# A two-layer encoder trunk on one core: first weight in two halves, some LayerNorm work on ScalarE, another order of head groups, and a table of priority shifts

## The chip, the cores and the metric

The kernel runs on one core of a Trainium2 chip. A core has a matmul engine (TensorE, PE in the profile), an elementwise engine (VectorE, DVE), an activation engine (ScalarE, ACT), a general engine (GpSimd, POOL) and an engine that here only issues DMAs (SyncE, SP). Each engine works through its own queue of instructions in order, and the engines wait for each other by semaphores. Matmul results land in PSUM, everything else lies in SBUF. The metric is the device time of one execution in microseconds (us); less is better.

## The reference

The input x is 512 rows (tokens) of 1024 values, in float32. After one LayerNorm come two layers, each with three kinds of attention side by side and a gated MLP:

```python
proj = x @ w_in                                   # 1024 x 4608
# differential softmax attention: 4 heads, two softmaxes of width 64 each,
#   rotary on 16 of 64 dims; o = (p0 - lam * p1) @ v, then rms_norm
# HGRN2 gated linear recurrence: 4 heads, 128 x 128 state, forward and backward,
#   summed, rms_norm, times silu(gate)
# cross-attention into 256 memory rows: 4 heads of 128
mix = jnp.concatenate([da_o, hg_o, mx_o], axis=-1) @ w_out
x = layer_norm(DEEPNORM_ALPHA * x + mix, ln1_g, ln1_b)
u = depthwise_conv_centred(x @ w_up, conv_w, conv_b)   # width 3 over the rows
gate, val = jnp.split(u, 2, axis=-1)
x = layer_norm(DEEPNORM_ALPHA * x + (jax.nn.silu(gate) * val) @ w_down, ln2_g, ln2_b)
```

The output is the 512 x 1024 result of the second layer.

## The kernel before

**Matmuls.** A float32 operand is split into a high and a low float16 part, and a product is three float16 matmuls (`mm3`: high x high, high x low, low x high). x lies transposed in `xh` and `xl` (8 blocks of 128 channels by 512 rows), the residual row-wise in four tiles `z[0]` to `z[3]` of 128 rows each.

**Weights.** `prep` brings one weight tile (1 MB, for the MLP's up-projection 512 KB) into SBUF: a DMA into one of two buffers `wst` (L302, or L300 in two pieces), the sum of squares on ScalarE (L307), a matmul with ones into a column of `stat` (L168), a power of two from the result's exponent on VectorE (`we`, `ws`, `wi`: L155 to L159), the scaled high part on ScalarE (`wh`, L310) and the low part on VectorE (`wl`, L311). The buffer `wst` is free when L311 is done, and only then the DMA of the next weight but one starts.

**Start.** `START` gives the order: constants, the first LayerNorm's gain and bias, the four tiles of x, two weights. `first_norm` takes each tile's mean and variance on VectorE (`norm`, L227 and L229), adds epsilon on GpSimd (L231), raises to the power -0.5 on GpSimd (L232) and normalises the tile on VectorE (L258). Then, for each block of 128 channels, four transposes on PE (L262), gain and bias on ScalarE (L264), high part and low part on VectorE (L265, L266). The first projection (`step_i`, the recurrence's values) has eight blocks of high-part matmuls, and then the matmuls with the weight's low part.

**A layer.** Head groups are worked on as pairs of heads: `hg` (recurrence), `mx` (memory) and `da` (differential), two pairs each. `SEQ` lists the order in which their projections and output projections are written into the program. Attention itself runs beside that in "lanes", stepped by the matmul time that the main line has used: recurrence and differential pairs share lane 0, memory pairs have lane 1. `rope_step` does the rotary part of the differential queries and keys on VectorE (L1003 to L1009). Output projections add into z through L569 (eviction of a PSUM bank, on VectorE). The last output projections are those of the memory pairs and of the second differential pair, and each finished row tile goes through `layernorm` (statistics L227 and L229, epsilon and power on GpSimd L231 and L232, L280 and L281 on VectorE, transposes L288, parts L292 and L293). The MLP runs in groups of up to four 128-column pairs, and after the last group `layernorm` runs again. With `idx == 4` (the last one) its result goes to the output by DMA (L283) instead of to transposes.

**Order.** The program is traced once, and `make_plan` reads its instructions, in the order in which they were written. `extract` finds what each depends on, and gives it a cost from a table of formulas; `deadlines` gives each a priority: a matmul the matmul time written before it, any other instruction the latest time at which those behind it can still be on time. The first `FIRST` DMAs come ahead of all. `simulate` then lists the instructions engine by engine: whenever an engine is free, the ready instruction with the smallest priority goes next. The program is traced a second time with these orders and with the buffers that the plan chose. The chip runs exactly these queues.

Of the kernel before, what the change touches and what calls it, by code (L numbers as in the profile page):

```python
# [10 lines left out]
F32 = mybir.dt.float32  # L11
F16 = mybir.dt.float16
# [27 lines left out]
MX_COST = 0.8  # L40
MX_EARLY = 4
START = "c0123wv"
_seq = [("hg", 0), ("rope",), ("hg", 1), ("mx", 0), ("mx", 1), ("da", 0), ("out", "hg", 0), ("da", 1), ("out", "hg", 1), ("out", "da", 0)]
SEQ = [_seq, _seq]
LANE = {"hg": 0, "da": 0, "mx": 1}
LAST = ("da", 1)
# [49 lines left out]
def trunk(ctx: ExitStack, tc: tile.TileContext, a, out, slots=None):  # L96
# [117 lines left out]
    qin = cp.tile([P, DEPTH], F32, name="qin")  # L214
    mkin = cp.tile([P, 2], F32, name="mkin")

    def load_x(t):
        nc.sync.dma_start(z[t], a["x"][0, t * P : (t + 1) * P, :])

# [2 lines left out]

    def norm(t, idx):
        zt = z[t]
        st = small(12, "bnst")
        for j in range(2):
            V.bn_stats(st[:, j * 6 : (j + 1) * 6], zt[:, j * 512 : (j + 1) * 512])  # L227
        mv = small(2, "bnmv")
        V.bn_aggr(mv, st)  # L229
        rs = small(1, "lnrs")  # L230
        G.tensor_scalar(rs, mv[:, 1:2], LN_EPS / (ALPHA * ALPHA if idx else 1.0), None, ALU.add)  # L231
        G.tensor_tensor(rs, rs, mhalf[:, 0:1], ALU.pow)  # L232
        return mv[:, 0:1], rs

# [20 lines left out]
    def first_norm():  # L255
        for t in range(TT):
            mu, rs = norm(t, 0)
            V.tensor_scalar(z[t], z[t], mu, rs, ALU.subtract, ALU.mult)  # L258
        for k in range(KT):
            pt = ptr()  # L260
            for t in range(TT):
                T.transpose(pt[:, t * P : (t + 1) * P], z[t][:, k * P : (k + 1) * P], ident)  # L262
            w = tmp([P, S], "w2", bufs=4)
            A.activation(w, pt, AF.Identity, scale=gbc[:, 0, k : k + 1], bias=gbc[:, 1, k : k + 1])  # L264
            V.tensor_scalar(xh[:, k, :], w, 1.0, None, ALU.mult)  # L265
            V.tensor_tensor(xl[:, k, :], w, xh[:, k, :], ALU.subtract)  # L266

# [24 lines left out]
                A.activation(xhs, pv, AF.Identity, scale=lnsc[:, idx : idx + 1])  # L292
                V.scalar_tensor_tensor(xls, pv, lnsc[:, idx : idx + 1], xhs, ALU.mult, ALU.subtract)  # L293

    def prep(src, shape):
        st = slot(wp, [P] + shape, F32, "wst", 2)
        if isinstance(src, tuple):
            w = shape[1] // len(src)
            for i, s_ in enumerate(src):
                nc.sync.dma_start(st[:, :, i * w : (i + 1) * w], s_)  # L300
        else:
            nc.sync.dma_start(st, src)  # L302
        n = shape[0] * shape[1]
        flat = st.rearrange("p a b -> p (a b)")
        h = slot(wp, [P] + shape, F16, "wh", 4)
        ss = small(1, "wss")
        A.activation(h.rearrange("p a b -> p (a b)").bitcast(BF16), flat, AF.Square, accum_out=ss)  # L307
        s, inv = pow2_scales(ss, 1, "w")
        l = slot(wp, [P] + shape, F16, "wl", 4)
        A.activation(h.rearrange("p a b -> p (a b)"), flat, AF.Identity, scale=s)  # L310
        V.scalar_tensor_tensor(l.rearrange("p a b -> p (a b)"), flat, s, h.rearrange("p a b -> p (a b)"), ALU.mult, ALU.subtract)  # L311
        return Weight(h, l, inv)

    def mm3(o, wh, wl, dh, dl, first, last, wt):
# [201 lines left out]
    def rms(o, eps=None):  # L516
        sq = tmp([P, 4, P], "w2", bufs=4)
        A.activation(sq, o.rearrange("p (c v) -> p c v", c=4), AF.Square)
        ss = small(4, "rmss")
        V.tensor_reduce(ss, sq, AX.X, ALU.add)  # L520
        rs = small(4, "rmrs")
        if eps is None:
            G.tensor_scalar(rs, ss, 1.0 / P, RMS_EPS, ALU.mult, ALU.add)
        else:
            G.tensor_tensor(rs, ss, eps, ALU.add)
        G.tensor_tensor(rs, rs, mhalf, ALU.pow)
        on = tmp([P, 4, P], "w2", bufs=4)
        V.tensor_tensor(on, o.rearrange("p (c v) -> p c v", c=4), rs.unsqueeze(2).broadcast_to([P, 4, P]), ALU.mult)
        return transposes(on)
# [66 lines left out]
    def emit():  # L596
        order = [(si, wi) for si, st in enumerate(steps) for wi in range(len(st[0]))]
        ready = {}
        at = [0]

        def prep_until(n):
            while at[0] < min(n, len(order)):
                si, wi = order[at[0]]
                spec = steps[si][0][wi]
                ready[si, wi] = prep(spec, [KT, 256] if isinstance(spec, tuple) else list(spec.shape[1:]))
                at[0] += 1

        done = set()
        cur = [None] * len(lanes)
        credit = [0.0] * len(lanes)  # L610

        def unit_step(i):
            if cur[i] is None:
                if not lanes[i] or not all(x in done for x in lanes[i][0][2]):
                    return None
                name, fn, _ = lanes[i].pop(0)
                cur[i] = (name, fn())
            try:
                return next(cur[i][1])
            except StopIteration:  # L620
                done.add(cur[i][0])
                cur[i] = None
                return 0.0

        def pump(dt):
            for i in range(len(lanes)):
                credit[i] += dt
                while credit[i] > 0:
                    c = unit_step(i)
                    if c is None:  # L630
                        credit[i] = 0.0
                        break
                    credit[i] -= c

        for op in START:
            if op == "c":
                ln_columns()
            elif op in "wv":
                prep_until("wv".index(op) + 1)
            else:  # L640
                load_x(int(op))
        seen = 0
        for si, (specs, fn, name, needs) in enumerate(steps):
            for x in needs:
                while x not in done:
                    if all([unit_step(i) is None for i in range(len(lanes))]):
                        raise RuntimeError(f"{x} can not run yet")
            seen += len(specs)
            prep_until(seen + AHEAD if specs else seen)
            t0 = pe_time[0]  # L650
            g = fn([ready.pop((si, wi)) for wi in range(len(specs))])
            if g is not None:
                for _ in g:
                    dt = pe_time[0] - t0
                    pump(dt)
                    t0 = pe_time[0]
            pump(pe_time[0] - t0)
            if name is not None:
                done.add(name)
# [32 lines left out]
    def build_layer(l):  # L692
# [55 lines left out]
        def hg_units(pr):  # L748
# [57 lines left out]
            def hg_attn():  # L806
# [31 lines left out]
                while m < S:  # L838
                    nb = S // m
                    for j in range(2):  # L840
                        Q, K, At, Dg, Tm = Qs[j], Ks[j], As[j], Ds[j], Ts[j]
                        p_ = psc()
                        if m <= 16:
# [7 lines left out]
                            V.copy_predicated(Dg, mk, p_[:, 0:P].rearrange("p (c t) -> p c t", c=4))  # L851
                            if m == 16:
                                for b in range(4):
                                    G.tensor_copy(diag_block(At, 32 * b, 32 * b, 32), Dg[32 * b : 32 * b + 32])
                        elif m <= 64:
                            for c in range(4):
                                for b in range(P // m):
# [364 lines left out]


class Op:
    __slots__ = ("i", "name", "eng", "cost", "tail", "reads", "writes", "table", "preds", "succs", "tiles", "dmab", "line", "kind", "small", "order_ins", "mv", "istr", "half", "mode")


def cost_of(i, kind, eng, outs, ins):
# [56 lines left out]
def extract(instrs):  # L1285
    ops = []
    last_half = None
    for i in instrs:
# [26 lines left out]
            o.cost, o.tail = cost_of(i, kind, o.eng, outs, ins)  # L1315
        o.reads = [b for b in ins if type(b.tensor).__name__ == "Tile"]
        o.writes = [b for b in outs if type(b.tensor).__name__ == "Tile"]
        o.preds, o.succs = set(), []
        o.small = _n(outs[0].ap) <= 16 if outs else False
        o.half = None  # L1320
        if o.eng == "PE":
# [42 lines left out]
    for o in ops:  # L1364
        o.tiles = []
        for wr, bs in ((False, o.reads), (True, o.writes)):
            for b in bs:
                t = b.tensor
                nm = t.name
                if nm not in tiles:  # L1370
                    tiles[nm] = t
                if nm not in o.tiles:
                    o.tiles.append(nm)
                psum = "PSUM" in str(t.space)
                p0, p1, m = region(b)
                h = hist[nm]
                for (j, w2, a0, a1, m2) in h:
                    if (wr or w2) and j != o.i:
                        if psum or (a0 < p1 and p0 < a1 and m & m2):
                            o.preds.add(j)  # L1380
        for wr, bs in ((False, o.reads), (True, o.writes)):
            for b in bs:
                p0, p1, m = region(b)
# [2 lines left out]
                if wr:  # L1386
                    if psum:
                        h[:] = []
                    else:
                        h[:] = [e for e in h if not (p0 <= e[2] and e[3] <= p1 and (e[4] & ~m) == 0 and e[0] != o.i)]  # L1390
                h.append((o.i, wr, p0, p1, m))
    for o in [o for o in ops if o.dmab][:FIRST]:
        o.dmab *= FAST
    gang, of = [], []
# [22 lines left out]
def simulate(ops, tiles, prio, fixed=None, wait=0.0, log=None):  # L1417
# [6 lines left out]
    free = {e: 0.0 for e in ("PE", "DVE", "ACT", "POOL", "SP")}  # L1424
    table = 0
    mode = 128
    dma_free = 0.0

    users = defaultdict(list)
    for o in ops:  # L1430
# [53 lines left out]
    while done < N:  # L1484
# [58 lines left out]
        order[e].append(i)  # L1543
        done += 1
        for s in o.succs:
            lat = LAT if ops[s].eng != o.eng else (0.03 if e != "PE" else -o.tail)
            if ops[s].eng == "POOL" and e != "POOL":
                lat += 0.12
            r = end[i] + lat
# [13 lines left out]
    return max(end), start, end, order, slot_of  # L1563


PEN = 20.0
SHARE = 0.35
TURN = 4.0
FIRST = 9
FAST = 205 / 370.0  # L1570


def deadlines(ops, tiles):
# [31 lines left out]
        D[i] = d  # L1605
    for k, o in enumerate([o for o in ops if o.dmab][:FIRST]):
        D[o.i] = k - 1000.0
    return [T[o.i] if o.eng == "PE" else D[o.i] for o in ops]


def make_plan(instrs):
# [48 lines left out]
```

## Time and profile before

| what | value |
|---|---|
| median of 3 runs | 1492.83 us (1492.78 to 1493.38) |
| the profiled execution, its own time | 1492.88 us |
| its span, first to last instruction | 1491.1 us |
| granted TensorE clock, mean | 0.997 of full |
| HBM read, written | 138.24 MB, 2.10 MB (94 GB/s over the span) |

The difference between time and span, 1.78 us, lies before the first and behind the last instruction. In the profile a group of instructions is named by engine, line, and the tiles that it writes and reads (`wl<-wst,ws,wh`). A row of the timeline begins with the start and the duration in us, and ends, in brackets, with the idle time before it and what ended it. A row of the windows view has the stretch, its length, and the busy time and number of instructions of each engine in it, then the granted clock, the DMA engines' busy share and GB/s. The page's 40 slices show VectorE's load over the span, in tenths:

```profile
DVE  7989968978997677666785978789888777566777
ACT  5876655666376556455466656566645656455550
```

### The profile page before, as it was taken

To read this page: it belongs to the slowest core of one execution; us is meant where nothing else is said; L and a number is where in the kernel's file an instruction comes from. 1 tells how busy PE (TensorE), PEld (TensorE's weight loads), DVE (VectorE), ACT (ScalarE), POOL (GpSimd) and SP (SyncE) were. 2 spreads that over 40 slices of the span, in tenths; PEclk is the share of its full clock that TensorE was granted. 3 is DMA by queue.
4 is the path that set the end of the run, shared out by engine and by line. 5 is a ranking of instruction groups with operands and counts; after the bars stand their busy time and mean duration, and the time that the engine had idled before them with its cause. 6 is when DMAs were issued, how large, how long until landed. Compare 5 with 4: busy or idle time off the path is not lost. (4 is left out here: it accounts for less than half of the span.)

```text
span 1491.1 us, 24496 instructions
## 1 busy us (share of the span) xinstructions
PE 1451.7 (97%) x9978; PEld 811.9 (54%) x9978; DVE 1168.4 (78%) x2242; ACT 865.1 (58%) x1094; POOL 130.1 (9%) x154
## 2 busy tenths in 40 slices
PE   6999999999999999999999999999999999999997
PEld 4566675565564444444487475655656544444443
DVE  7989968978997677666785978789888777566777
ACT  5876655666376556455466656566645656455550
POOL 1001020000111101001000101001001101001011
PEclk9999999999999999999999999999999999999999
DMA  6342111223143323232324202112232323333221
GB/s 238 114 150 86 59 58 59 101 71 101 46 143 114 107 85 113 85 113 96 128 90 140 87 30 86 57 57 77 79 100 85 113 88 118 99 92 114 86 84 57
DMA packets 158171, 141.91 MB, mean 95 GB/s; under 512 B 3302, under 2 KB 139114, under 8 KB 158058
## 3 DMA queue, kind: packets, MB, share of 16 engines
q1 hardware_dynamic: 158058, 140.35, 29.2%
q8 instruction: 78, 1.28, 0.3%
q14 instruction: 35, 0.29, 0.1%
HBM read 138.24 MB, written 2.10 MB: 94 GB/s over the span
## 5 line engine op out<-in xcount | busy, mean ns | idle before, releaser
L140 PEld LDWEIGHTS <-wh 128*128 128x128 f16 x2624 | 251.0, 98 | 237.5 <-issue 3.4
L311 DVE SCALAR_TENSOR_TENSOR wl<-wst,ws,wh 128x2048 f16<-128x2048 f32 x122 | 312.5, 2561 | 52.3 <-ACT wh L310 51.4
L140 PE MATMUL mm<-xh,wl 128*128 128x512 f16 (+1 forms) x832 | 305.3, 367 | 0.6 <-DVE wl L311 0.6
L140 PE MATMUL mm<-xh,wh 128*128 128x512 f16 (+1 forms) x832 | 305.2, 367 | 0.0
L140 PE MATMUL mm<-xl,wh 128*128 128x512 f16 (+1 forms) x832 | 305.0, 367 | 0.0
L307 ACT ACTIVATE wh<-wst 128x2048 bf16<-128x2048 f32 x122 | 232.2, 1903 | 102.4 <-PE stat L168 49.2
L310 ACT ACTIVATE wh<-wst,ws 128x2048 f16<-128x2048 f32 x122 | 243.5, 1996 | 40.1 <-DVE ws L157 19.5
L140 PE MATMUL mm<-wh,t 128*128 128x512 f16 (+1 forms) x768 | 223.5, 370 | 0.0
L140 PEld LDWEIGHTS <-wl 128*128 128x128 f16 x1312 | 128.2, 98 | 123.0 <-DVE wl L311 0.9
L140 PEld LDWEIGHTS <-t 128*128 128x128 f16 x1152 | 110.2, 98 | 121.4 <-issue 0.6
L569 DVE SCALAR_TENSOR_TENSOR z<-mm,inv,z 128x512 f32<-128x512 f32 x176 | 130.2, 745 | 45.9 <-PE mm L140 32.2
L140 PE MATMUL sc<-xl,wh 128*128 128x512 f16 (+1 forms) x416 | 147.5, 355 | 0.0
L140 PE MATMUL sc<-xh,wl 128*128 128x512 f16 (+1 forms) x416 | 147.5, 355 | 0.0
L140 PE MATMUL sc<-xh,wh 128*128 128x512 f16 (+1 forms) x416 | 147.5, 355 | 0.0
L140 PE MATMUL mm<-wl,t 128*128 128x512 f16 (+1 forms) x384 | 142.1, 370 | 0.0
L155 DVE TENSOR_SCALAR we<-stat 128x1 int32<-128x1 int32 x122 | 18.6, 153 | 118.8 <-PE stat L168 118.6
L1151 POOL TENSOR_TENSOR t<-f 128x512 f32<-128x512 f32 x44 | 60.6, 1378 | 542.7 <-DVE f L1149 438.6
L140 PE MATMUL mm<-wh,mgh 128*128 128x512 f16 x192 | 73.3, 382 | 4.7 <-DVE z L569 4.7
L1147 ACT ACTIVATE f<-sc,cvb,cw 128x512 f32<-128x512 f32 x44 | 34.1, 775 | 71.4 <-PE stat L168 69.3
L140 PE MATMUL mm<-wh,mgl 128*128 128x512 f16 x192 | 72.9, 381 | 0.9 <-DVE mgl L547 0.6
L140 PE MATMUL mm<-wl,mgh 128*128 128x512 f16 x192 | 73.3, 382 | 0.0
L1042 ACT ACTIVATE f<-sc,dam,iqk 128x512 f32<-128x512 f32 x64 | 49.3, 774 | 38.8 <-DVE dam L1040 34.3
(244 smaller groups left out, 2125.4 us busy)
## 6 DMA issues: line engine op xcount, KB each, us to landing
wst<-in_w_up_dram SPq DMA_DIRECT2D x88, 512.0 KB, 4.3
wst<-in_w_in_dram SPq DMA_DIRECT2D x36, 1024.0 KB, 4.8
wst<-in_w_down_dram SPq DMA_DIRECT2D x22, 1024.0 KB, 4.9
wst<-in_w_out_dram SPq DMA_DIRECT2D x12, 1024.0 KB, 4.9
wst<-in_w_mem_kv_dram SPq DMA_DIRECT2D x8, 1024.0 KB, 5.0
z<-in_x_dram SPq DMA_DIRECT2D x4, 512.0 KB, 4.9
mix<-in_ln_g_dram SPq DMA_DIRECT2D x4, 512.0 KB, 3.6
mix<-in_ln_b_dram SPq DMA_DIRECT2D x4, 512.0 KB, 4.7
```

Of the source, the lines that this page charges most:

```text
L140: T.matmul(o, lhsT, rhs, start=start, stop=stop)
L155: V.tensor_scalar(e, tot.bitcast(I32), 0x7F000000, 1, ALU.bitwise_and, ALU.logical_shift_right)
L307: A.activation(h.rearrange("p a b -> p (a b)").bitcast(BF16), flat, AF.Square, accum_out=ss)
L310: A.activation(h.rearrange("p a b -> p (a b)"), flat, AF.Identity, scale=s)
L311: V.scalar_tensor_tensor(l.rearrange("p a b -> p (a b)"), flat, s, h.rearrange("p a b -> p (a b)"), ALU.mult, ALU.subtract)
L569: V.scalar_tensor_tensor(zs, p_, ivs[half % len(ivs)], zs, ALU.mult, ALU.add)
L1042: A.activation(pe[:, c, :], sc_[c], AF.Exp, bias=mx[:, c : c + 1], scale=iqk, accum_out=z1 if c else z0)
L1147: A.activation(c, p_, AF.Identity, scale=cw[:, 1, v : v + 1], bias=cvb[:, l, i + 22 * v : i + 22 * v + 1])
L1151: G.tensor_tensor(gt[:, n, :], c2[:, 0, :], c2[:, 1, :], ALU.mult)
```

## The change

- The first weight is brought in by `prep_parts` in two halves of four blocks each: two DMAs, two sums of squares (their matmuls add up in one column of `stat`), two scaled high parts, two low parts. `FIRST` goes from 9 to 10 for it.
- `ACT_TILES = 1`: tile `z[0]` is normalised on ScalarE, with a small VectorE instruction for its bias.
- `ACT_STATS = (0, 0, 0, 0, 3)`: in the last LayerNorm the sum and the centred sum of squares of tiles 0 to 2 come from two ScalarE passes with accumulation instead of VectorE's L227 and L229.
- The epsilon additions of `norm` and `rms` go from GpSimd to VectorE. The copies of the recurrence's 32 x 32 blocks (L854) go from GpSimd to ScalarE. `DVE_BLOCKS` is empty and so does nothing. An ACTIVATE on a constant (`warm`) is written at the start.
- `SEQ`: the projections of the differential pairs come ahead of those of the memory pairs, and the output projections behind both.
- The planner: reads of one PSUM tile by one engine keep their order (`soft`); the DMA engines are taken to be free from 2.1 us on; and `deadlines` adds a table `NUDGE` of some 300 entries. An entry `(engine, a, b, d)` adds d us to the priority of that engine's instructions among those numbered a to b.

```diff
+FIRST_PARTS = 2
+ACT_TILES = 1
+ACT_STATS = (0, 0, 0, 0, 3)
+DVE_BLOCKS = ()
-_seq = [("hg", 0), ("rope",), ("hg", 1), ("mx", 0), ("mx", 1), ("da", 0), ("out", "hg", 0), ("da", 1), ("out", "hg", 1), ("out", "da", 0)]
+_seq = [("hg", 0), ("rope",), ("hg", 1), ("da", 0), ("da", 1), ("mx", 0), ("mx", 1), ("out", "hg", 0), ("out", "hg", 1), ("out", "da", 0)]
...
+    warm = cp.tile([P, 4], F32, name="warm")
+    A.activation(warm, mhalf, AF.Square)
...
     def norm(t, idx):
         zt = z[t]
+        if t < ACT_STATS[idx]:
+            sm = small(12, "bnst")
+            scr = tmp([P, D], "sg", BF16, bufs=2)
+            A.activation(scr, zt, AF.Identity, accum_out=sm[:, 0:1])
+            mu = sm[:, 2:3]
+            V.tensor_scalar(mu, sm[:, 0:1], 1.0 / D, None, ALU.mult)
+            nm_ = sm[:, 3:4]
+            V.tensor_scalar(nm_, sm[:, 0:1], -1.0 / D, None, ALU.mult)
+            A.activation(scr, zt, AF.Square, bias=nm_, accum_out=sm[:, 1:2])
+            rs = small(1, "lnrs")
+            V.tensor_scalar(rs, sm[:, 1:2], 1.0 / D, LN_EPS / (ALPHA * ALPHA if idx else 1.0), ALU.mult, ALU.add)
+            G.tensor_tensor(rs, rs, mhalf[:, 0:1], ALU.pow)
+            return mu, rs
...
-        G.tensor_scalar(rs, mv[:, 1:2], LN_EPS / (ALPHA * ALPHA if idx else 1.0), None, ALU.add)
+        V.tensor_scalar(rs, mv[:, 1:2], LN_EPS / (ALPHA * ALPHA if idx else 1.0), None, ALU.add)
...
             mu, rs = norm(t, 0)
-            V.tensor_scalar(z[t], z[t], mu, rs, ALU.subtract, ALU.mult)
+            if t < ACT_TILES:
+                nb = small(1, "gss")
+                V.scalar_tensor_tensor(nb, mu, -1.0, rs, ALU.mult, ALU.mult)
+                A.activation(z[t], z[t], AF.Identity, bias=nb, scale=rs)
+            else:
+                V.tensor_scalar(z[t], z[t], mu, rs, ALU.subtract, ALU.mult)
...
+    def prep_parts(st, src, shape, parts):
+        n = shape[0] // parts
+        flat = lambda t, i: t[:, i * n : (i + 1) * n].rearrange("p a b -> p (a b)")
+        h = slot(wp, [P] + shape, F16, "wh", 4)
+        ss = small(parts, "gbto", bufs=1)
+        tot = stat[:, nstat[0] % 512 : nstat[0] % 512 + 1]
+        nstat[0] += 1
+        for i in range(parts):
+            nc.sync.dma_start(st[:, i * n : (i + 1) * n], src[:, i * n : (i + 1) * n])
+            A.activation(flat(h, i).bitcast(BF16), flat(st, i), AF.Square, accum_out=ss[:, i : i + 1])
+            T.matmul(tot, ones, ss[:, i : i + 1].bitcast(BF16)[:, 1:2], start=i == 0, stop=i == parts - 1)
+        s, inv = pow2_of(tot, 1, "w")
+        l = slot(wp, [P] + shape, F16, "wl", 4)
+        for i in range(parts):
+            A.activation(flat(h, i), flat(st, i), AF.Identity, scale=s)
+            V.scalar_tensor_tensor(flat(l, i), flat(st, i), s, flat(h, i), ALU.mult, ALU.subtract)
+        return Weight(h, l, inv)
...
-            G.tensor_scalar(rs, ss, 1.0 / P, RMS_EPS, ALU.mult, ALU.add)
+            V.tensor_scalar(rs, ss, 1.0 / P, RMS_EPS, ALU.mult, ALU.add)
         else:
-            G.tensor_tensor(rs, ss, eps, ALU.add)
+            V.tensor_tensor(rs, ss, eps, ALU.add)
...
-                                    G.tensor_copy(diag_block(At, 32 * b, 32 * b, 32), Dg[32 * b : 32 * b + 32])
+                                    A.activation(diag_block(At, 32 * b, 32 * b, 32), Dg[32 * b : 32 * b + 32], AF.Identity)
...
+                    elif psum and j != o.i and ops[j].eng == o.eng:
+                        o.soft.add(j)
...
+    for o in ops:
+        o.soft -= o.preds
+        o.preds |= o.soft
...
-    dma_free = 0.0
+    dma_free = 2.1
...
-            lat = LAT if ops[s].eng != o.eng else (0.03 if e != "PE" else -o.tail)
+            lat = LAT if ops[s].eng != o.eng else (0.03 if e != "PE" and i not in ops[s].soft else -o.tail)
...
+NUDGE = (
+    (1, 8510, 8576, 7.1), (1, 8458, 8542, -8.72), (1, 2085, 2163, -4.07), (0, 3376, 3460, -26.71), (1, 7787, 7798, -15.33), (0, 3415, 3420, -1.56),
...
+    (0, 9744, 9753, 1.17), (0, 6158, 6353, 0.65), (0, 6309, 6320, 1.02),
+)
...
-FIRST = 9
+FIRST = 10
...
-    return [T[o.i] if o.eng == "PE" else D[o.i] for o in ops]
+    D = [T[o.i] if o.eng == "PE" else D[o.i] for o in ops]
+    for e, a, b, d in NUDGE:
+        for o in ops[a:b]:
+            if o.eng == ("PE", "DVE", "ACT", "POOL", "SP")[e]:
+                D[o.i] += d
+    return D
```

More of the change, by code (lines that the diff above doesn't have):

```diff
@@ L263, in first_norm @@
             w = tmp([P, S], "w2", bufs=4)
-            A.activation(w, pt, AF.Identity, scale=gbc[:, 0, k : k + 1], bias=gbc[:, 1, k : k + 1])
+            if k in DVE_BLOCKS:
+                V.tensor_scalar(w, pt, gbc[:, 0, k : k + 1], gbc[:, 1, k : k + 1], ALU.mult, ALU.add)
+            else:
+                A.activation(w, pt, AF.Identity, scale=gbc[:, 0, k : k + 1], bias=gbc[:, 1, k : k + 1])
             V.tensor_scalar(xh[:, k, :], w, 1.0, None, ALU.mult)
@@ L293, in layernorm, with prep @@
                 V.scalar_tensor_tensor(xls, pv, lnsc[:, idx : idx + 1], xhs, ALU.mult, ALU.subtract)
-    def prep(src, shape):
+    def prep(src, shape, parts=1):
         st = slot(wp, [P] + shape, F32, "wst", 2)
+        if parts > 1:
+            return prep_parts(st, src, shape, parts)
         if isinstance(src, tuple):
@@ L604, in prep_until @@
                 spec = steps[si][0][wi]
-                ready[si, wi] = prep(spec, [KT, 256] if isinstance(spec, tuple) else list(spec.shape[1:]))
+                ready[si, wi] = prep(spec, [KT, 256] if isinstance(spec, tuple) else list(spec.shape[1:]), FIRST_PARTS if at[0] == 0 else 1)
                 at[0] += 1
@@ L1224 @@
 class Op:
-    __slots__ = ("i", "name", "eng", "cost", "tail", "reads", "writes", "table", "preds", "succs", "tiles", "dmab", "line", "kind", "small", "order_ins", "mv", "istr", "half", "mode")
+    __slots__ = ("i", "name", "eng", "cost", "tail", "reads", "writes", "table", "preds", "succs", "tiles", "dmab", "line", "kind", "small", "order_ins", "mv", "istr", "half", "mode", "soft")
 def cost_of(i, kind, eng, outs, ins):
@@ L1317, in extract @@
         o.writes = [b for b in outs if type(b.tensor).__name__ == "Tile"]
-        o.preds, o.succs = set(), []
+        o.preds, o.succs, o.soft = set(), [], set()
         o.small = _n(outs[0].ap) <= 16 if outs else False
```

48 rows, old and new, of the table NUDGE are left out of this document.

## The prediction

> **What bounds the kernel now.** I read the page's engine shares first, then cut the span into stages with the windows view, then asked in the view of waits what TensorE (PE) stood for.
>
> ```profile
> span 1491.1 us, 24496 instructions
> ## 1 busy us (share of the span) xinstructions
> PE 1451.7 (97%) x9978; PEld 811.9 (54%) x9978; DVE 1168.4 (78%) x2242; ACT 865.1 (58%) x1094; POOL 130.1 (9%) x154
> ```
>
> PE is the bound: 9978 matmuls that no part of the diff removes. What an order can win is PE's idle time, 1491.1 - 1451.7 = 39.4 us, and the stretches in which PE runs at a lower clock. Next, where that idle time lies:
>
> ```profile
> core 0: us, PE busy (x) PEld busy (x) DVE busy (x) ACT busy (x) POOL busy (x), PEclk, DMA share, GB/s
> 0.00:20.07 20.07, 5.30 (x20) 3.40 (x21) 13.03 (x41) 8.56 (x9) 3.83 (x14) 1.00 0.86 318
> 20.07:410.00 389.93, 382.83 (x3245) 236.53 (x3245) 341.16 (x750) 251.34 (x377) 27.65 (x40) 1.00 0.27 87
> 410.00:800.00 390.00, 390.00 (x2153) 207.64 (x2151) 280.20 (x457) 226.16 (x223) 34.06 (x30) 1.00 0.35 111
> 800.00:1119.00 319.00, 313.62 (x2770) 190.40 (x2769) 267.82 (x580) 191.87 (x304) 23.67 (x34) 1.00 0.23 74
> 1119.00:1128.00 9.00, 6.34 (x27) 3.48 (x25) 7.23 (x17) 2.64 (x4) 1.77 (x2) 0.81 0.00 0
> 1128.00:1479.26 351.26, 351.08 (x1762) 169.51 (x1760) 250.80 (x390) 184.52 (x179) 36.59 (x30) 1.00 0.31 96
> 1479.26:1491.10 11.84, 2.55 (x12) 0.98 (x10) 8.20 (x13) 0.00 (x0) 2.49 (x4) 0.74 0.29 110
> ```
>
> Stretch minus PE busy gives: start 14.77, layer 0's projections and attention 7.10, its MLP 0.00, layer 1's attention 5.38, a hole at layer 1's first LayerNorm 2.66, the second MLP 0.18, tail 9.29; together 39.4. So the 741 us of the two MLPs can give nothing, and the sum has four terms: start, tail, hole, attention.
>
> **Start (first weight in halves, one x tile on ScalarE).** PE's longest wait is here, and what ends it is VectorE's normalising of x:
>
> ```profile
> PE tr L262 <- DVE z L258: 8.8, 4, 4.7
> ```
>
> The steps in order are ScalarE's (ACT) and then VectorE's (DVE) and PE's rows of the timeline:
>
> ```profile
> 12.08 1.91 ACT L307 ACTIVATE wh<-wst 128x2048 bf16<-128x2048 f32 x1 [10.08 <-DMA wst<-in_w_in_dram]
> 13.89 0.19 ACT L307 ACTIVATION_READ_ACCUMULATOR wh<-wst 128x1 f32 x1
> 14.80 1.91 ACT L307 ACTIVATE wh<-wst 128x2048 bf16<-128x2048 f32 x1 [0.72 <-DMA wst<-in_w_in_dram]
> 16.61 0.19 ACT L307 ACTIVATION_READ_ACCUMULATOR wh<-wst 128x1 f32 x1
> 16.71 1.43 ACT L264 ACTIVATE w<-tr,gbc 128x512 f32<-128x512 f32 x2
> 18.03 1.99 ACT L310 ACTIVATE wh<-wst,ws 128x2048 f16<-128x2048 f32 x1
> ```
>
> ```profile
> 12.42 2.59 DVE L258 TENSOR_SCALAR z<-z,bnmv,lnrs 128x1024 f32<-128x1024 f32 x3
> ...
> 15.06 0.69 PE L262 MATMUL tr<-cst,z 128*128 128x128 f32 x2 [0.20 <-DVE z L258]
> ...
> 15.13 0.15 DVE L157 TENSOR_SCALAR ws<-we 128x1 int32<-128x1 int32 x1
> ...
> 17.50 0.43 DVE L265 TENSOR_SCALAR xh<-w 128x512 f16<-128x512 f32 x1
> ...
> 20.07 0.37 PE L140 MATMUL mm<-wh,xh 128*128 128x256 f16 x1 [0.59 <-ACT wh L310]
> ```
>
> The two weights land 14.80 - 12.08 = 2.72 us apart, so a half lands about 1.36 earlier, at 10.7 (an estimate). Its squares take half of 1.91 plus 0.19 = 1.15; those of the second half start at 12.08 and end at 13.2. From the end of the sum (14.08) to the end of the scale on DVE (15.28) pass 1.20 us, so the scale is there at 14.4 and a scaled half (1.99/2) at 15.4. On the x side the last tile is normalised at 15.01; one tile of three on ACT instead (2.59/3 = 0.86) makes it 14.2, and transposes (0.69) 14.9. ACT then does L264 (0.72) to 16.1, DVE L265 (0.43) to 16.6, and with two hand-overs the first matmul stands at about 16.8 instead of 20.07: 3.3. I take **-3.0**. If ACT keeps the second weight's squares (1.91 + 0.19) ahead of L264, 1.2 is left; the low end is 0: the new ACTIVATE on z waits for POOL's power, and behind it in ACT's queue stand the squares of the first half, for which the scale waits. The gain stays only if nobody is late next; DVE, at 341 of 390 us in the stretch behind, is the one to watch.
>
> The ACTIVATE `warm` loads its table while ACT waits for data until 12.08: nothing. Split in two, the first load has one issue more on SP's queue, whose data the full DMA engines (share 0.86) carry no faster.
>
> **Tail (statistics of three tiles on ScalarE, the epsilon on VectorE).**
>
> ```profile
> 1481.85 0.75 DVE L569 SCALAR_TENSOR_TENSOR z<-mm,inv,z 128x512 f32<-128x512 f32 x1
> 1482.52 0.74 DVE L281 SCALAR_TENSOR_TENSOR z<-z,lnrs,mix 128x512 f32<-128x512 f32 x1
> 1483.17 0.69 DVE L227 BATCH_NORM_STATS2 bnst<-z 128x6 f32<-128x512 f32 x1
> 1483.78 0.74 DVE L281 SCALAR_TENSOR_TENSOR z<-z,lnrs,mix 128x512 f32<-128x512 f32 x1
> 1484.43 0.20 DVE L229 BATCH_NORM_AGGREGATE bnmv<-bnst 128x2 f32<-128x12 f32 x1
> 1484.67 1.41 DVE L280 SCALAR_TENSOR_TENSOR z<-z,bnmv,mix 128x512 f32<-128x512 f32 x2
> 1484.72 0.78 POOL L231 TENSOR_SCALAR lnrs<-bnmv 128x1 f32<-128x1 f32 x1 [4.54 <-DVE bnmv L229]
> 1485.59 0.93 POOL L232 TENSOR_TENSOR lnrs<-lnrs,mhalf 128x1 f32<-128x1 f32 x1
> 1486.54 1.41 DVE L281 SCALAR_TENSOR_TENSOR z<-z,lnrs,mix 128x512 f32<-128x512 f32 x2 [0.46 <-POOL lnrs L232]
> ```
>
> Behind the last eviction (L569) DVE still does two L281 of tile 2, then tile 3 goes through DVE, POOL twice and DVE. L231 on DVE costs about 0.15 (the row of L157) in place of 0.87 from 1484.72 to 1485.59: -0.7. The statistics of tiles 0 to 2 leave DVE (six L227), so that one of tile 2's two L281 (0.65) may come before the last eviction: -0.5 of it. But ACT's way is longer. The nearest rows are the squares of a LayerNorm row, and two such passes come one behind the other:
>
> ```profile
> L181 ACT ACTIVATE sg<-mix 128x1024 bf16<-128x1024 f32 x8 | 8.4, 1051 | 17.1 <-DMA mix<-in_ln_b_dram 15.1 <-DMA mix<-in_ln_g_dram 2.0
> ...
> L181 ACT ACTIVATION_READ_ACCUMULATOR sg<-mix 128x1 f32 x8 | 1.5, 188 | 0.0
> ```
>
> 2 x (1.05 + 0.19) = 2.5 us before tile 2 has its scale. Ends: -2.0 when both L281 go ahead of the last eviction, +0.6 when both end up behind tile 3 (1.3 - 0.7). I take **-1.2**. ACT is idle in this stretch (0.00), so nothing queues behind these passes.
>
> **The hole (order alone).** PE stands at layer 1's output projection because DVE does two whole LayerNorms before the eviction that frees PE's bank:
>
> ```profile
> 1122.40 0.74 DVE L569 SCALAR_TENSOR_TENSOR z<-mm,inv,z 128x512 f32<-128x512 f32 x1
> ...
> 1123.20 0.58 PE L140 MATMUL mm<-wh,mgh 128*128 128x512 f16 x1 [2.66 <-DVE z L569]
> ```
>
> The window of 9.00 us around it has a granted clock of 0.81, another 9.00 x 0.19 = 1.7 us. With it the hole costs 4.4. The table moves priorities, and with the statistics' epsilon on DVE the wait for POOL in it is shorter; the two LayerNorms remain, so I take **-3.0**, ends -4.4 and 0. The Trainium skill (TensorE: Matmul & The Clock Gate, Part 1) states that the clock falls to half after an idle window of some 3.4 us; read as a limit on one gap, a gap of 2.66 would cost no clock, the hole would be worth 2.7 at most and the sum's gain would be at least 0.3 smaller. This trace speaks against that reading: the clock is down right behind 2.66 us.
>
> **Attention (differential pairs ahead of memory pairs, the table, small steps between engines).** 7.10 + 5.38 = 12.5 us of idle PE, in many waits of under 1.4 us. The pairs' projections change places: the same matmuls, and the weights of 1 MB trade places on SP's queue, with a DMA share of 0.27 behind them. What it may bring: differential attention, which now ends the layer with few matmuls beside it, gets the memory projections beside it. The 32 copies that go from POOL to ACT are priced by ACT's own row of that shape, and DVE's load where the pairs move to by the row of that stretch:
>
> ```profile
> L862 ACT ACTIVATE t<-sc 32x128 f32<-32x128 f32 (+1 forms) x48 | 14.6, 304 | 7.0 <-PE sc L140 6.3
> ```
>
> ```profile
> 100.00:200.00 100.00, 98.36 (x1213) 61.19 (x1211) 96.77 (x223) 67.09 (x95) 15.23 (x20) 1.00 0.25 81
> ```
>
> 32 x 0.304 = 9.7 us on ACT lie beside PE's work, as ACT is at 251 of 390: nothing, and up to 9.7 if the score matmuls behind them are late. The 36 epsilon additions (0.15 each, 5.4 on DVE over both layers) shorten a chain each by some tenths, and stay in this term. I take a quarter of the idle time, **-3.0**: a plan of this kind left these 12.5 once, and its new order will have waits of its own. Ends: -8, and +10.7 by the first rival.
>
> **Sum.** -3.0 - 1.2 - 3.0 - 3.0 = -10.2. The profiled execution took 1492.88 us around its span of 1491.1, within 0.05 of the median of 1492.83: 1492.9 - 10.2 = **1482.7**.
>
> **Rivals.**
>
> *VectorE overloaded in layer 0 (slower).* The projections that move forward carry rotary steps on DVE, five operations a head:
>
> ```profile
> L1003 DVE STREAM_SHUFFLE sg<-mm 128x512 f32<-128x512 f32 x16 | 11.7, 730 | 0.0
> ```
>
> The other four are of the same 512 columns; at 0.69 (L227 above) a head is 3.5 and a pair's four heads 13.9 us, put into a recurrence in which DVE has 100 - 96.77 = 3.2 free. If all of it delays evictions, PE waits 10.7 more; the lead from the start is lost there too, as DVE and not PE then sets the pace, and hole and tail stay at -4.2: +6.5, 1499.4. It decides from 7.2 us of new waits on. For it: 96.77. Against it: the evictions can go ahead of the recurrence, whose work can wait, and the light memory projections follow.
>
> *The order brings nothing on the chip.* Start and tail come, hole and attention stay: -4.2, 1488.7. For it: the kernel's own planner made the present order too, and the hole was left.
>
> *The start is lost again as well.* ACT takes the second weight first (-1.2), the tail gives -0.5, the rest 0: 1491.2, no measurable change.
>
> *Nearly everything goes.* Start -3.3, tail -2.0, hole -4.4, attention -7: 1476.2. For it: the MLP stretches show PE without any idle time at all.
>
> **Chances.** Forecast 0.45, order brings nothing 0.20, start lost as well 0.12, nearly everything 0.13, VectorE overloaded 0.10. A measurement of this kernel can tell about 0.2% (3 us) from no change: faster 0.78, same 0.12, slower 0.10. The range leaves out the slower case, half of the 1491.2 case (0.06) and the far end of the best one (0.03): 1474.5 to 1491.5.
>
> **What would show it.** Start: the first fp16 matmul at 16 to 18 us; at 18.9 the second weight's squares went first. Tail: from the last L569 to the end of the span some 8 us instead of 9.2, with no POOL row but the power. Hole: no wait of PE over 1 us between layer 1's output projection and its MLP, and a granted clock of 1.00 there. Attention: PE idle under 10 in the two stretches together. Wrong: DVE over 96% and PE waiting for L1005 or L569 between 100 and 250 us, or a new hole of 2 us and more.

## The result, and the profile after

| | median | lowest to highest | against before, ratio and 95% interval |
|---|---|---|---|
| before | 1492.80 us | 1492.62 to 1493.38 | |
| changed | 1482.38 us | 1481.14 to 1483.18 | 0.9929 [0.9912, 0.9946] |

The forecast was 1482.7, and faster. The profiled execution of the changed kernel is the quickest of its four (1481.14), 11.7 us below that of before; the numbers worked out below from these two profiles add up to that, and not to the median's 10.4. One of the ten executions of experiment e2 (below) took 2540.43 us, at a mean clock of 0.559, and is left out of its numbers.

The page of the changed kernel, span and engines:

```profile
span 1479.4 us, 24491 instructions
PE 1444.8 (98%) x9979; PEld 809.9 (55%) x9979; DVE 1159.8 (78%) x2276; ACT 880.3 (60%) x1143; POOL 104.4 (7%) x86
```

PE's idle time fell from 39.4 to 34.6 us only. The other 7 us are in its busy time: a matmul that is issued at half the clock counts as busy, and so does the longer interval from a matmul over 128 rows to one over 64 (0.31 us in the kernel before, against 0.22 to the next of its own shape). The stages by the windows view, cut where the same work ends in both (columns as before):

```profile
core 0: us, PE busy (x) PEld busy (x) DVE busy (x) ACT busy (x) POOL busy (x), PEclk, DMA share, GB/s
0.00:17.69 17.69, 4.31 (x20) 3.79 (x21) 11.44 (x40) 7.40 (x11) 3.14 (x10) 1.00 0.89 310
17.69:280.00 262.31, 258.94 (x2561) 168.26 (x2560) 238.96 (x547) 189.21 (x277) 6.88 (x6) 1.00 0.29 96
280.00:410.00 130.00, 127.29 (x723) 71.26 (x722) 109.27 (x228) 69.38 (x121) 7.89 (x6) 0.99 0.25 79
410.00:800.00 390.00, 389.08 (x2121) 204.68 (x2119) 277.23 (x461) 225.24 (x224) 40.50 (x26) 1.00 0.36 109
800.00:1105.00 305.00, 299.78 (x2727) 184.86 (x2725) 259.06 (x575) 195.18 (x318) 8.44 (x8) 1.00 0.23 75
1105.00:1467.50 362.50, 362.50 (x1826) 175.94 (x1825) 255.58 (x415) 192.70 (x194) 35.60 (x28) 1.00 0.31 94
1467.50:1479.36 11.86, 2.92 (x14) 1.13 (x12) 8.31 (x15) 1.19 (x2) 1.97 (x2) 0.72 0.36 133
```

Idle time of PE: start 13.38 (14.77 before), layer 0's attention 3.37 + 2.71 = 6.1 (7.1), its MLP 0.9 (0), layer 1's attention with its first LayerNorm 5.2 (8.0). The wait of 2.66 us at that LayerNorm is gone.

Busy time hides part of the gain, so I also worked out a curve of **lost time** from the traces: PE's instructions in order of start, for each the median interval from a start of its shape to the next start (0.216 us for 512 columns in fp16, for example), and the time minus the sum of these. Only differences between its columns and rows mean anything. Read at marks where both orders have done the same work, in us, with the experiments of the next section:

```
mark                  before changed  e1    e3    e4    e5    e6    e7    e11   e12
first projection       20.3   16.5   17.1  16.7  19.9  19.3  16.5  16.4  17.8  16.7
layer 0, in its MLP    40.7   37.8   39.2  39.2  44.7  40.8  38.3  39.1  39.8  32.3
layer 1, in its MLP    64.0   52.6   61.8  62.3  69.1  59.1  52.9  57.0  58.5  45.8
end of the span        73.4   61.7   70.9  71.8  78.6  68.5  62.0  66.1  67.6  54.9
```

Before against changed: the start gives 3.8, layer 0's attention takes 0.9 back (2.9 ahead at the second mark), layer 1's attention with its LayerNorm gives 8.5 (11.4 ahead), the tail 0.3. So nearly three quarters come from one stretch of layer 1. Each column is one execution, and the clock makes executions differ: e5 has PE's order of the kernel before until 1118 us and stands 1.0 us lower at the first mark, and the 0.9 that layer 0 gives back holds a stretch at half clock (366.9 to 370.3 us in the changed kernel) that cost 1.7 and that the kernel before didn't have there.

### The profile page after: what moved, and what is told of

The parts are those of the page before. It is cut to its first block, busy times and chain, and to the rows that moved or that the text cites. A ratio compares the mean times of both kernels' runs of the same rounds, so it can differ in the third digit from the quotient of the medians.

```text
span 1479.4 us, 24491 instructions
## 1 busy us (share of the span) xinstructions
PE 1444.8 (98%) x9979; PEld 809.9 (55%) x9979; DVE 1159.8 (78%) x2276; ACT 880.3 (60%) x1143; POOL 104.4 (7%) x86
## 4 chain that ended last, share of the span: by engine, by line
PE 91%; DVE 5%; ACT 2%; issue 1%; DMA 0%; POOL 0%; SPq 0%; DVEq 0%; ACTq 0%; POOLq 0%
PE mm L144 62%; PE sc L144 21%; PE tr L144 5%; PE tr L561 2%; DVE t L929 1%; PE tr L316 1%; DVE wl L341 1%; PE tr L1016 0%; DVE t L933 0%; ACT wh L337 0%; DVE bnst L247 0%; PE tr L287 0%; ACT wh L340 0%; DVE z L617 0%; PE tr L427 0%
## 5 line engine op out<-in xcount | busy, mean ns | idle before, releaser
L341 DVE SCALAR_TENSOR_TENSOR wl<-wst,ws,wh 128x2048 f16<-128x2048 f32 x121 | 298.0, 2463 | 52.1 <-ACT wh L340 51.8
L144 PE MATMUL mm<-wh,t 128*128 128x512 f16 (+1 forms) x768 | 227.1, 370 | 0.0
L1199 POOL TENSOR_TENSOR t<-f 128x512 f32<-128x512 f32 x44 | 66.0, 1501 | 534.6 <-DVE f L1197 301.9
L159 DVE TENSOR_SCALAR we<-stat 128x1 int32<-128x1 int32 x122 | 18.7, 154 | 99.7 <-PE stat L172 98.4
L144 PE MATMUL mm<-wh,xh 128*128 128x256 f16 x240 | 65.4, 274 | 0.0
L144 PE MATMUL mm<-wh,xl 128*128 128x256 f16 x240 | 65.2, 273 | 0.0
```

Source lines behind the costliest of these rows:

```text
L144: T.matmul(o, lhsT, rhs, start=start, stop=stop)
L159: V.tensor_scalar(e, tot.bitcast(I32), 0x7F000000, 1, ALU.bitwise_and, ALU.logical_shift_right)
L1199: G.tensor_tensor(gt[:, n, :], c2[:, 0, :], c2[:, 1, :], ALU.mult)
```

## The experiments

Each was measured beside runs of the kernel before on the same chip, and the gains of e1 to e5 are worked out from the ratio to these. e1 to e4, e5 to e8, and e9 to e12 ran on three different chips (the kernel before: 1492.61, 1492.89 and 1492.86 us). Every edit lets the planner make all queues anew.

**e1: the table emptied.**

```diff
-NUDGE = ( ... 293 entries ... )
+NUDGE = ()
```

> The changed kernel with an empty table of priority shifts; every other edit stays. If the table carries the order's gain (theory): the start's gain stays (first fp16 matmul before 18.5 us), the hole of over 2 us at layer 1's first LayerNorm or one like it is back, and the time is 1487 to 1491. If the edits alone carry it (rival A): 1481 to 1484. If the table repairs a loss that the new order of head groups brings (rival B): over 1494.

1490.48 us, 0.9986 [0.9977, 0.9995]. The table carries the order's gain: without it some 2 us are left of 10.4. By the curve the start keeps its lead (17.1; first fp16 matmul at 17.52), and layer 1 falls back to 61.8 from 52.6. The hole doesn't come back as one wait: around layer 1's output projections and LayerNorm no wait of PE is over 1.2 us. View of waits, 1060 to 1150 us:

```profile
PE mm L144 <- DVE mgh L593: 1.2, 1, 1.2
PE tr L172 <- DVE gss L588: 1.2, 1, 1.2
PE mm L144 <- DVE z L617: 1.2, 1, 1.2
PE mm L144 <- DVE mgl L595: 0.8, 1, 0.8
PE sc L144 <- ACT xh L320: 0.8, 1, 0.8
PE tr L316 <- DVE z L309: 0.6, 1, 0.6
```

The first, second and fourth of these stand in the changed kernel too; the other three, 2.6 us together, don't.

**e2: the table emptied, and the old order of head groups.**

```diff
-_seq = [..., ("hg", 1), ("da", 0), ("da", 1), ("mx", 0), ("mx", 1), ("out", "hg", 0), ...]
+_seq = [..., ("hg", 1), ("mx", 0), ("mx", 1), ("da", 0), ("out", "hg", 0), ("da", 1), ...]
 NUDGE = ()
```

> As the run without the table, and with the old order of head groups (memory pairs ahead of differential pairs). Theory: the order of groups alone is worth little, so within 2.5 us of the run without the table, 1486 to 1491. Rival B (the new order overloads VectorE in layer 0 and eats the start's lead there): 3 us or more faster than the run without the table, with the lead still there at 280 us.

1490.83 us (the median of nine), 0.9999 [0.9989, 1.0008]. That is 0.3 us from e1 by the medians and 1.9 by the ratios, and the two intervals overlap: with the other edits, the order of groups by itself is worth nothing that can be told from zero. e2's executions fall into two groups, five from 1490.55 to 1490.83 at a mean clock of 0.998 or 0.999, and four from 1492.52 to 1495.97 at 0.995 or 0.996.

**e3: the start's edits alone, on the kernel before** (`FIRST_PARTS`, `prep_parts`, `ACT_TILES`, `FIRST = 10`, as in the diff above).

> The kernel before with the start's edits alone (first weight in halves, z[0] normalised on ScalarE, FIRST = 10). Theory: first fp16 matmul at 17 to 18.5 instead of 20.07 and the lead is kept to the end, 1489 to 1490.5. Rival (the lead is lost in layer 0's attention, where VectorE is full): the start as early, and the time 1492 to 1493.5.

1491.20 us, 0.9987 [0.9978, 0.9997]: 1.9 us, between the kept lead and the rival. The first fp16 matmul starts at 17.14, and the lost time at the first mark is 3.6 less; at the second mark 1.5 is left. Most of the difference is TensorE's clock. The same waits (the longest, 1.3 us, for L1051's line) stand in both kernels, and they end 2.3 us apart in time; the windows around them, in the kernel before and in e3:

```profile
342.00:352.00 10.00, 7.57 (x41) 2.98 (x40) 9.56 (x24) 9.02 (x15) 0.00 (x0) 1.00 0.18 57
```

```profile
340.00:350.00 10.00, 7.87 (x35) 3.12 (x34) 9.26 (x23) 8.96 (x15) 0.00 (x0) 0.83 0.19 58
```

In e3 the granted clock is 0.83 of 10.00 us, 1.7 us lost; in the kernel before it stays full, with as much idle time (2.1 against 2.4). The other executions of e3 bear this out: four took 1489.70 to 1489.99 us at a mean clock of 0.997, inside my range for a kept lead, and six took 1491.15 to 1491.87 at 0.996, the profiled one (1491.26) among them.

**e4: the new order of head groups alone, on the kernel before.**

```diff
-_seq = [("hg", 0), ("rope",), ("hg", 1), ("mx", 0), ("mx", 1), ("da", 0), ("out", "hg", 0), ("da", 1), ("out", "hg", 1), ("out", "da", 0)]
+_seq = [("hg", 0), ("rope",), ("hg", 1), ("da", 0), ("da", 1), ("mx", 0), ("mx", 1), ("out", "hg", 0), ("out", "hg", 1), ("out", "da", 0)]
```

> The kernel before with the new order of head groups alone. Theory: layer 0 loses some us between 100 and 250 us and wins them back at the output projections (300 to 350), so 1490 to 1495. Rival (order of groups is the main gain): 1484 to 1488. Rival B (VectorE overloaded): over 1496.

1497.92 us, 1.0038 [1.0023, 1.0053]: slower by 5.7, on the side of the rival "VectorE overloaded", but not at its place. Between 100 and 280 us PE's listed waits are 2.6 us in all. The loss of layer 0 stands at the output projections; view of waits, 355 to 385 us, and the windows row:

```profile
PE tr L168 <- DVE gss L540: 1.9, 1, 1.9
PE mm L140 <- DVE mgh L545: 1.5, 1, 1.5
PE mm L140 <- DVE z L569: 1.4, 1, 1.4
```

```profile
355.00:385.00 30.00, 25.25 (x106) 10.70 (x105) 21.81 (x37) 14.28 (x15) 0.00 (x0) 0.89 0.43 127
```

`gss` and `mgh` are the split of the memory pairs into two fp16 parts: a sum of squares on ScalarE, a sum on VectorE, a matmul, a scale, the high part. With the memory pairs last, nothing else is written beside this chain. PE waits 3.4 us for it and 1.4 for an eviction (z), and the clock of 0.89 costs another 3.3 (30.00 x 0.11). The kernel before waits nearly as long there, in shorter pieces (PE idle 4.8 us from 280 to 410 us, 5.3 in e4), but at the full clock. So most of the 4.0 us that e4 loses by the second mark is the clock.

**e5: evictions ahead of the LayerNorm, on the kernel before.** The only edit is in `deadlines`; the numbers are those of layer 1's output projections.

```diff
+    ev = [o.i for o in ops if o.eng == "DVE" and "mm_" in " ".join(o.tiles) and any(x.startswith("z") for x in o.tiles) and 9300 < o.i < 9900]
+    for i in ev:
+        D[i] -= 6.0
     return [T[o.i] if o.eng == "PE" else D[o.i] for o in ops]
```

> The kernel before, with the priority of VectorE's evictions in layer 1's last output projections lowered by 6 us, so that they go ahead of the LayerNorm work there; nothing else. Theory: the wait of 2.66 us at 1120 us is gone and the clock stays at full speed there, so 4.4 us less in that stretch and 1488 to 1490 in all. Rival by the skill's limit on a gap: no clock to win, 2.7 us at most. Rival (the LayerNorm behind is late instead): 1491 to 1493.

1488.20 us, 0.9968 [0.9956, 0.9980]: 4.8 us from one priority. In e5's profile the stretch that had a clock of 0.81 has no gap and the full clock:

```profile
1119.00:1128.00 9.00, 9.00 (x50) 4.84 (x48) 8.80 (x19) 3.48 (x4) 1.36 (x2) 1.00 0.01 2
```

50 matmuls and transposes in these 9 us instead of 27. The hole cost its 2.66 and the clock behind it: between the second and the third mark e5 loses 5.0 us less than the kernel before (18.3 against 23.3).

**e6: the table's entries for layer 1 alone; e7: those for TensorE alone.**

```diff
-    for e, a, b, d in NUDGE:
+    for e, a, b, d in [n for n in NUDGE if n[1] >= 6200]:      # e6
+    for e, a, b, d in [n for n in NUDGE if n[0] == 0]:         # e7
```

> The changed kernel with the table's entries for layer 1 alone (instructions numbered 6200 and up). By the two traces, layer 1's attention and its first LayerNorm hold some 7 us of the table's gain and layer 0 some 1.5: 1483 to 1485.5. Rival (both layers alike): 1486 to 1487.5.

> The changed kernel with the table's entries for TensorE alone (131 of 293). If the table's gain comes from TensorE's order (which matmuls fill a wait): 1483 to 1486. If it comes from VectorE's and ScalarE's order (evictions, small chains): 1488 to 1491.

e6: 1482.38 us, 0.9930 [0.9916, 0.9945], all of the changed kernel's time; better than I gave it. The entries for layer 0 give nothing that can be measured. e7: 1486.05 us, 0.9956 [0.9939, 0.9973], just above the first of my two cases: TensorE's order alone is a bit over half of the table's 8 us, the rest needs the entries of the other engines with it. What those give alone was not run.

**e8: the last LayerNorm's statistics on VectorE again; e9: its epsilon on GpSimd again.**

```diff
-ACT_STATS = (0, 0, 0, 0, 3)
+ACT_STATS = (0, 0, 0, 0, 0)                                     # e8
-        V.tensor_scalar(rs, mv[:, 1:2], LN_EPS / (ALPHA * ALPHA if idx else 1.0), None, ALU.add)
+        (G if idx == 4 else V).tensor_scalar(rs, mv[:, 1:2], LN_EPS / (ALPHA * ALPHA if idx else 1.0), None, ALU.add)   # e9
```

> The changed kernel with the last LayerNorm's statistics on VectorE again (ACT_STATS all 0). Theory: the tail is 0.3 to 1 us longer from the last eviction to the end, total 1482.5 to 1483.5. Rival (tile 3's chain alone sets the end): the same tail within 0.2 us.

> The changed kernel with the last LayerNorm's epsilon addition on GpSimd again. Theory: this addition and not ScalarE's statistics is what shortened the tail, so from the last eviction to the end 9.2 us instead of 8.7. Rival (the order of the last instructions did it): 8.7 still.

e8: 1481.89 us, 0.9927 [0.9912, 0.9942]; e9: 1482.25 us, 0.9927 [0.9907, 0.9947]. The medians can't tell these apart from the changed kernel; the tails can. Timeline rows and spans: the changed kernel's (span 1479.4 above), then e8's, then e9's.

```profile
1470.64 0.74 DVE L617 SCALAR_TENSOR_TENSOR z<-mm,inv,z 128x512 f32<-128x512 f32 x1
1471.30 0.74 DVE L309 SCALAR_TENSOR_TENSOR z<-z,lnrs,mix 128x512 f32<-128x512 f32 x1
1471.96 0.69 DVE L247 BATCH_NORM_STATS2 bnst<-z 128x6 f32<-128x512 f32 x1
1472.57 0.73 DVE L309 SCALAR_TENSOR_TENSOR z<-z,lnrs,mix 128x512 f32<-128x512 f32 x1
...
1473.45 0.15 DVE L251 TENSOR_SCALAR lnrs<-bnmv 128x1 f32<-128x1 f32 x1
...
1473.69 0.99 POOL L252 TENSOR_TENSOR lnrs<-lnrs,mhalf 128x1 f32<-128x1 f32 x1 [3.22 <-DVE lnrs L251]
1474.84 1.41 DVE L309 SCALAR_TENSOR_TENSOR z<-z,lnrs,mix 128x512 f32<-128x512 f32 x2
```

```profile
1471.18 0.74 DVE L617 SCALAR_TENSOR_TENSOR z<-mm,inv,z 128x512 f32<-128x512 f32 x1
...
core 0: 1479.9 us, clock 0.997
```

```profile
1470.87 0.75 DVE L617 SCALAR_TENSOR_TENSOR z<-mm,inv,z 128x512 f32<-128x512 f32 x1
...
1473.74 0.78 POOL L251 TENSOR_SCALAR lnrs<-bnmv 128x1 f32<-128x1 f32 x1 [3.04 <-DVE bnmv L249]
1474.60 0.93 POOL L252 TENSOR_TENSOR lnrs<-lnrs,mhalf 128x1 f32<-128x1 f32 x1
...
core 0: 1480.1 us, clock 0.995
```

From the last eviction to the end: 9.2 us before, 8.7 in the changed kernel, 8.7 in e8, 9.2 in e9. The epsilon on VectorE is the tail's whole gain. The statistics on ScalarE give nothing: tile 2's two steps (the two L309) still come behind the last eviction and around tile 3's statistics, as in the kernel before.

**e10: 37 entries in place of 293.** 36 of the 293 are kept and one is new; the planner's own total stays the same.

> The changed kernel with a table of 37 entries in place of 293: most entries are dropped, and the planner's own total stays the same. Theory: most entries move nothing that counts, and the time stays within 1.5 us of the changed kernel, 1481 to 1484. Rival (the entries work together): 1485 or more.

1483.06 us, 0.9931 [0.9917, 0.9946], as the changed kernel. Most of the table moves nothing that counts.

**e11: the second differential pair's output projection ahead of the memory pairs', empty table; e12: the same with a table of its own, found by the same kind of search over the planner.** This follows from e4 and from the changed kernel, which has the same chain in both layers. Its waits between 1080 and 1100 us:

```profile
PE mm L144 <- DVE mgh L593: 1.2, 1, 1.2
PE tr L172 <- DVE gss L588: 1.2, 1, 1.2
PE mm L144 <- DVE mgl L595: 0.8, 1, 0.8
```

```diff
...
-        add(wrows(w_out, 1024, 4), out_mx, None, [(l, "mx", 1)])
-        lg = LAST
-        add(wout(*lg), out_last, None, [(l, *lg)])
+        def out_last(ws):
+            load_ln(1 + 2 * l)
+            mx = down_part(ws, state["s", ("mx", 0)], 4)
+            for t in range(TT):
+                for half in range(2):
+                    mx(half, t)
+                    yield
+                layernorm(t, 1 + 2 * l)
+
+        add(wout(*LAST), lambda ws: down(ws, state["s", LAST], 2), None, [(l, *LAST)])
+        add(wrows(w_out, 1024, 4), out_last, None, [(l, "mx", 1)])
...
-NUDGE = ( ... 293 entries ... )
+NUDGE = ()                                  # e11
+NUDGE = (                                   # e12: 54 entries
+    (0, 3376, 3460, -26.71), (1, 125, 131, 1.59), (1, 9492, 9678, -5.77), (2, 8359, 8443, -11.24), (0, 9409, 9465, -1.56), (0, 9437, 9454, -26.2),
...
+)
```

> As the run with the empty table, and the second differential pair's output projection is written ahead of the memory pairs', which alone run beside the LayerNorm. Theory: the three waits of TensorE for the split of the memory pairs (some 3.2 us in each layer) get this projection beside them and go, two thirds of it stays won: 1484 to 1488 against 1490.5. Rival (the LayerNorm has fewer matmuls beside it and waits as long): 1489 to 1492.

> The run before it with a table of its own of 54 entries, found for it by the same kind of search. Theory: as the table of the change was worth 8 us on the chip, most of the same comes on top: 1475 to 1480, faster than both kernels. Rival (what the planner sees beyond here the chip does not follow): 1481 to 1485.

e11: 1486.80 us, 0.9958 [0.9943, 0.9973], 3.7 below e1 by the medians (4.2 by the ratios), which has the same empty table and the other order. The waits for the split, 6.4 us in e1's profile, are gone, but those for evictions of z grew from 2.5 (3 waits) to 6.3 (9 waits). Much of the gain is the clock: e1 drops to half in both layers (368.5 to 371.9 and 1098.9 to 1102.4 us), e11 nowhere between its start and its tail, and the mean clock is 0.996 in all ten executions of e1 and 0.998 in all four of e11. e12: **1475.18 us**, 0.9881 [0.9865, 0.9898]: 17.7 below the kernel before and 7.2 below the changed one. Its attention stretches:

```profile
0.00:410.00 410.00, 393.28 (x3343) 247.68 (x3344) 363.73 (x831) 271.62 (x413) 15.54 (x22) 1.00 0.31 103
...
800.00:1140.00 340.00, 337.11 (x2956) 207.92 (x2955) 293.32 (x641) 207.94 (x333) 12.82 (x12) 1.00 0.24 76
```

PE idle 2.9 us from 800 to 1140, and 16.7 before 410, of which the start alone is 13.4 in the changed kernel. None of the three waits above is among e12's, and its clock is at 0.998 in all four executions.

## Why the prediction was right, step by step

The total and its direction were right, the terms only partly: the tail was too large, the hole too small, and a part of the start's gain was luck with the clock.

- **Start, forecast -3.0.** The lost time fell by 3.8, in another way than worked out. The first fp16 matmul came at 17.69, not 16.8, so it moved by 2.4. ScalarE's and PE's rows of the changed kernel show why:

```profile
10.97 1.06 ACT L353 ACTIVATE wh<-wst 128x1024 bf16<-128x1024 f32 x1 [8.74 <-DMA wst<-in_w_in_dram]
11.93 0.19 ACT L353 ACTIVATION_READ_ACCUMULATOR wh<-wst 128x1 f32 x1
12.03 1.23 ACT L281 ACTIVATE z<-z,gss,lnrs 128x1024 f32<-128x1024 f32 x1
13.16 1.04 ACT L353 ACTIVATE wh<-wst 128x1024 bf16<-128x1024 f32 x1
...
13.31 1.97 PE L287 MATMUL tr<-cst,z 128*128 128x128 f32 x8 [0.97 <-ACT z L281]
15.07 0.21 PE L354 MATMUL stat<-gbto,ones 128*128 128x1 bf16 x1
...
16.44 1.14 ACT L358 ACTIVATE wh<-wst,ws 128x1024 f16<-128x1024 f32 x1
...
17.69 0.42 PE L144 MATMUL mm<-wh,xh 128*128 128x256 f16 x1
```

  The first half's squares began at 10.97 (10.7 expected), but the new ACTIVATE on z[0] stood between the two halves' squares: the second began at 13.16 and not at 12.08. I had this ACTIVATE's place in the queue as the cause of the low end and not in the sum. Behind it the matmul of the second sum came only after eight transposes in PE's queue, at 15.07. What made up for it is the clock: in the first 5.00 us from the first fp16 matmul PE starts 28 instructions before and 43 in the changed kernel, which reaches full speed earlier (at 18.7 us, 1.0 after that matmul; in the kernel before at 24.1, 4.0 after it):

```profile
20.07:25.07 5.00, 5.00 (x28) 4.18 (x28) 5.00 (x8) 5.00 (x7) 0.00 (x0) 1.00 0.28 85
```

```profile
17.69:22.69 5.00, 5.00 (x43) 4.47 (x42) 5.00 (x10) 5.00 (x6) 0.00 (x0) 1.00 0.48 181
```

  (The view shows 1.00 there, as the trace has no record of the clock so early; the interval of 0.213 us between matmuls of 256 columns, twice the later one, shows half speed.) That part is luck in the main. e10 has the changed kernel's order on PE until 41.8 us and the same first matmul, and e5 the order of the kernel before; their first 5.00 us:

```profile
17.69:22.69 5.00, 5.00 (x32) 4.36 (x31) 4.54 (x9) 4.55 (x6) 0.00 (x0) 1.00 0.48 180
```

```profile
20.12:25.12 5.00, 5.00 (x38) 4.44 (x38) 5.00 (x8) 5.00 (x7) 0.00 (x0) 1.00 0.29 84
```

  So e10 starts 32 where the changed kernel starts 43, and e5 38 where the kernel before starts 28. Over all the traces half speed lasts 1.0 to 4.1 us behind the first fp16 matmul with the new start, and 1.9 to 4.0 with the old one.
- **Tail, forecast -1.2.** Mis-sized: 0.5 (9.2 to 8.7). The epsilon gave 0.5 where I had 0.7 (e9), the statistics 0 where I had 0.5 (e8).
- **Hole, forecast -3.0.** Right in mechanism, too small: alone it is worth 4.8 [3.0, 6.6] on the chip (e5), about the full 4.4 that the rows gave. But it isn't the table that closes it. e3, which changes the start alone, still has the wait (2.7); e1 and e2 have no table and no wait over 1.6 us there. With the other edits the plan breaks it into shorter waits, and the table removes those (2.6 us in e1).
- **Attention, forecast -3.0.** What is left of 11.7 after start 3.8, tail 0.3 and a hole of 4.4 is 3.2, but not as I split it: layer 0 gave 0.9 back, with a stretch at half clock of 1.7 in it, and layer 1 gave 4.1. My reason, that the memory projections would fill the end of differential attention, was half of it: they did, and the split of the memory pairs became the new wait at the end (1.2 + 1.2 + 0.3 in layer 0, 1.2 + 1.2 + 0.8 in layer 1), so that the new order is worth nothing measurable by itself (e1 against e2) and costs 5.7 without the other edits (e4). The table gained by ordering layer 1 (e6).
- **Rivals.** "VectorE overloaded" was wrong in place: DVE is 96% busy from 100 to 200 us in e4 (97% before), and PE is idle for 2.8 of these 100 us (1.6 before). "The order brings nothing" holds without the table (e1), not with it. "Nearly everything goes" is what e12 does, after another change of order.

## What to carry to other kernels

An order that a planner's model found is worth testing stretch by stretch: here 8 of 10.4 us came from the order of one layer, and one priority (evictions ahead of the LayerNorm work that can wait) was worth 4.8. Where the work that ends a stage has a chain over several engines (squares, sum, scale, split), write something independent beside it, and move it off the end before a search polishes the rest. A short edit ahead of a shared in-order queue (a tile on ScalarE between two halves of a weight) can take back part of what it brings (by the rows above, the first matmul came 2.4 us earlier and not 3.3). And where single edits are worth 1 to 2 us, look at the clock of every execution before calling a difference the edit's.

## What the runs showed of the hardware

TensorE's clock falls to half for 3.4 us at a time (a dip; twice as long, 6.8, once in e4 and once in e7), and this needs no single long gap. The Trainium skill (TensorE: Matmul & The Clock Gate, Part 1) describes a free-running window of 3.4 us, and warns of idle windows of about that length; the traces agree on the length (1123.2 to 1126.6 us in the kernel before, 366.9 to 370.3 in the changed kernel), but 2.66 us idle, and even waits of 1.2, 1.2 and 0.3 close together (the changed kernel's layer 0), were enough. Whether they are, changes between executions with the same order on PE. e5 has that of the kernel before until 1118 us, and the same waits of 1.3, 0.3, 0.3 and 0.2 between 342 and 352 us; the kernel before keeps the full clock there (1.00, shown at e3), and e5 doesn't:

```profile
342.00:352.00 10.00, 7.86 (x36) 2.92 (x36) 9.09 (x20) 8.73 (x15) 0.00 (x0) 0.83 0.23 67
```

The changed kernel at its two such places, the split of the memory pairs in each layer:

```profile
362.00:372.00 10.00, 7.29 (x28) 2.72 (x26) 8.79 (x18) 6.08 (x7) 0.00 (x0) 0.83 0.27 97
1088.00:1098.00 10.00, 6.76 (x32) 2.73 (x31) 9.36 (x22) 5.08 (x6) 0.00 (x0) 1.00 0.28 102
```

and e9 at the second of them, with the same two waits of 1.2 us:

```profile
1088.00:1098.00 10.00, 7.56 (x30) 2.77 (x29) 9.10 (x21) 5.20 (x6) 0.00 (x0) 0.83 0.28 105
```

Such a dip costs 1.7 us. It bears on small changes: e3's start was earlier by 3.6 us of lost time and kept 1.5 in its profile, as a dip at 344 us, which the kernel before had escaped, took 1.7. In e3 and e2 the groups of execution times go with the mean clock, as told there. The four runs of the changed kernel spread over 2.0 us, with 0.997 in three and 0.996 in the slowest; what decides whether a dip comes was not shown.
